# Attention of a hybrid decoder layer: probabilities transposed by TensorE into PSUM instead of by VectorE blocks and SBUF-to-SBUF transfers

## The chip, the cores and the metric

The kernel runs on one core of one Trainium2 chip. The metric is the device time of one execution in microseconds; the median of three runs before the change is 1390.19 us.

## What is computed

One decoder layer, float32, sequence 1024, width 1024, batch 1. The normalised input is projected to queries (8 heads of 64), to keys and values of 2 groups, to gates and to a convolution branch. Each head attends in three ways, and a gate weighs each of them:

```python
p_c = masked_softmax(s_c, dist_c >= 0)              # 63 compressed keys
o_c = jnp.einsum('bgrqn,bngd->bqgrd', p_c, vc)
...
p_s = masked_softmax(s_s, dist_s >= 0)              # selected blocks: all 16, so plain causal attention
o_s = jnp.einsum('bgrqnl,bgqnld->bqgrd', p_s, vs_sel)
...
p_w = masked_softmax(s_w, mask_w)                   # window of 512
o_w = jnp.einsum('bgrqs,bsgd->bqgrd', p_w, vwc)
o = gc[..., 0:1] * o_c + gc[..., 1:2] * o_s + gc[..., 2:3] * o_w
...
mix = jnp.concatenate([attn_out, conv_out], axis=-1) @ w_out
x = x + gate1 * mix
h2 = rms_norm(x, norm2) * (1 + scale2) + shift2
ff = jnp.square(jax.nn.relu(h2 @ w_ff1)) @ w_ff2
return x + gate2 * ff
```

The scores have the queries on the partitions, so the probabilities must be transposed before they can be multiplied with the values.

## The kernel before

All activations stand with channels on partitions and tokens along the columns, in two halves of 512 tokens. Every matmul operand is split into a high part rounded to fp32r and the remainder (`hi`, `lo`), and a product is three matmuls, `hi*hi + hi*lo + lo*hi` (`mm3`, L460). Weights are loaded in pieces of 256 KB into three staging buffers, cast by ScalarE or GpSimd and subtracted by VectorE (`weights`, L536).

No engine's order is written out by hand. Each helper of `Plan` (`mm` L305, `pet` L312, `copy` L330, `tt` L341, `dvt` L381, `dma` L388) records an operation with a cost in ns. `issue` (L272) runs a list scheduler over what was recorded: `_forward` (L154) places operations by priority on the engines and on one model of the DMA engines, `_backward` (L237) renews the priorities, and the best of eight passes is written out as each engine's fixed order. The plan's costs thus decide only the order; on the chip each engine takes its instructions in that order and waits where an operand is late. All plain transfers go through the SP queue, in order.

The first part (projections, compressed keys and values, conv and attention, output projection, the first 30 tiles of the MLP's first product for the first 512 tokens) is one such plan, the rest of the MLP a second one.

Attention goes in 12 steps (`supers`, L1172). A step is a pair of heads `hp` with query blocks `m` of 256 tokens: four steps with m = 0 and 1, then eight with m = 2 or 3. Within a step:

- `row` (L934), for each of 128 queries and a head: scores by TensorE into the banks `sc`, a table added and the maximum taken by VectorE (`ttr`, L373), exponentials by ScalarE, scaling by gate and denominator on GpSimd or ScalarE. Then `dvt` (L382) transposes 32x32 blocks on VectorE into the tile `Tt`.
- `shuffle` (L1011): 16 SBUF-to-SBUF transfers move the 32-row blocks from `Tt` to `Dt`, which completes the transpose. `Tt` and `Dt` exist once.
- `pv` (L1017): for pieces of `Dt` a ScalarE copy makes `hi` and a VectorE subtraction `lo` (both SBUF to SBUF); each matmul of values with probabilities covers both heads and, where causality allows, both query tiles, so most have 512 moving columns and the others 256. They sum in the bank `po` or `stb`. The result goes to `d_attn` in DRAM (`flush_pv`, L1174) and is read back by `load_mix` (L1101).

TensorE's other work while attention runs: the conv products (`conv_fills`, L1089) during the first four steps; then `first_half` (L1129), the output projection, second norm and first MLP product for the first 512 tokens. Its residual sum goes to `d_x1` in DRAM and is read back twice. After the last step the output projection of the second half follows, then its norm, then the second plan.

## Time and profile before

| | |
|---|---|
| median of 3 runs | 1390.19 us (1389.83 to 1394.37) |
| profiled execution, its own time | 1398.64 us |
| span from first to last instruction in that execution | 1396.7 us |
| mean granted TensorE clock | 0.955 |
| 0 to 225 us | projections, compressed keys, values, queries |
| 225 to 853 us | attention, with conv and the first half's products between |
| 853 us to the end | the MLP plan |

The profile is of one execution. Busy times of TensorE count a matmul from its start to the modelled end of its result, and matmuls overlap; what a matmul costs in a stream is read from the distance between starts. The granted clock is 1.0 at the higher of TensorE's two levels (2.4 GHz) and 0.5 at the lower (1.2 GHz); a value between is a mean over the stretch.

### The profile page before, as it was taken

The page shows a single profiled execution, that of the slowest core. Times are in us where ns is not written, and L with a number is a line of the kernel's source. Part 1 is how long each engine was busy: PE and PEld are TensorE (multiplying, and loading weights), DVE is VectorE, ACT ScalarE, POOL GpSimd, SP SyncE. Part 2 cuts the span into 40 slices and gives each one's busy share as a digit, 9 for nine tenths or more (in the row PEclk, how much of TensorE's full clock was granted, in tenths as well). Part 3 has the DMA queues.
Part 4 walks back from the last instruction along what each step waited for, and adds up shares of the span by engine and source line. Part 5 has one row for each costly group of instructions (what it writes and reads, how often), then busy time and mean ns, then how long its engine had stood idle before and what let it go on. Part 6 is the DMA issues. An engine that isn't in the chain of part 4 may idle for free.

```text
span 1396.7 us, 17048 instructions
## 1 busy us (share of the span) xinstructions
PE 1278.2 (92%) x5608; PEld 1031.4 (74%) x5608; DVE 835.7 (60%) x2019; ACT 619.0 (44%) x1206; POOL 131.2 (9%) x244
## 2 busy tenths in 40 slices
PE   6998999889878898987886997999999999999998
PEld 2777788668756777776765785878888888888887
DVE  6986969779778795776784647433432343143222
ACT  5775656646646475766673635411221032013200
POOL 0000003222312121212120000000000000000000
PEclk9999999889989999998988998999999999999999
DMA  9578866886686856879669714432321232122131
GB/s 327 174 195 226 262 216 208 213 197 177 192 222 172 247 165 185 231 186 222 173 165 258 225 46 157 126 124 76 106 91 61 68 114 63 58 91 91 31 121 61
DMA packets 110029, 220.66 MB, mean 158 GB/s; under 512 B 14841, under 2 KB 40994, under 8 KB 109428
## 3 DMA queue, kind: packets, MB, share of 16 engines
q1 hardware_dynamic: 106196, 204.76, 51.1%
q0 software_dynamic: 3744, 14.81, 3.7%
q8 instruction: 44, 0.72, 0.2%
q14 instruction: 45, 0.37, 0.1%
HBM read 151.77 MB, written 36.80 MB: 135 GB/s over the span
## 4 chain that ended last, share of the span: by engine, by line
PE 59%; DMA 14%; DVE 13%; SPq 7%; ACT 4%; issue 3%; POOL 0%; DVEq 0%; ACTq 0%; POOLq 0%
PE pd L310 37%; PE fa L310 10%; PE sc L310 9%; SPq L394 7%; DMA FA<-FA 5%; DVE RA L345 3%; DVE FA L382 3%; ACT FA L328 2%; PE stb L310 2%; DVE FA L356 2%; DVE FA L345 2%; DMA d_x<-FA 2%; DVE FA L375 1%; ACT RA L334 1%; PE po L310 1%
## 5 line engine op out<-in xcount | busy, mean ns | idle before, releaser
L334 ACT CAST RA<-FA 128x512 fp32r<-128x512 f32 (+4 forms) x323 | 231.5, 738 | 585.6 <-PE pd L310 286.3
L345 DVE TENSOR_TENSOR RA<-FA,RA 128x512 fp32r<-128x512 f32 (+5 forms) x407 | 319.7, 809 | 185.1 <-PE pd L310 95.0
L310 PE MATMUL fa<-RA 128*128 128x512 f32 (+1 forms) x1384 | 398.9, 407 | 18.2 <-DVE RA L345 8.0
L310 PE MATMUL sc<-RA 128*128 128x512 f32 (+6 forms) x1328 | 319.0, 368 | 22.5 <-DVE mx L375 8.9
L310 PE MATMUL pd<-hid,RA 128*128 128x512 f32 x1344 | 336.2, 389 | 0.0
L310 PEld LDWEIGHTS fa<-RA 128*128 128x128 f32 (+1 forms) x1384 | 267.1, 197 | 81.9 <-DVE RA L345 13.8
L310 PEld LDWEIGHTS pd<-hid,RA 128*128 128x128 f32 x1344 | 252.2, 188 | 52.2
L310 PEld LDWEIGHTS sc<-RA 128*128 128x128 f32 x1328 | 236.3, 194 | 70.9 <-DVE mx L375 12.1
L310 PE MATMUL pd<-RA 128*128 128x512 f32 x1008 | 263.9, 393 | 8.6 <-ACT RA L334 6.0
L310 PEld LDWEIGHTS pd<-RA 128*128 128x128 f32 x1008 | 189.8, 190 | 51.7 <-ACT RA L334 6.3
L356 DVE SCALAR_TENSOR_TENSOR FA<-pd,mod,FA 128x512 f32<-128x512 f32 x64 | 46.1, 745 | 201.1 <-PE pd L310 201.1
L382 DVE STREAM_TRANSPOSE FA<-FA 128x128 f32<-128x128 f32 (+8 forms) x224 | 97.4, 481 | 60.3 <-DMA FA<-FA 53.6
L328 ACT ACTIVATE FA<-FA,nm 128x64 f32<-128x64 f32 (+6 forms) x192 | 114.1, 596 | 23.2 <-DVE nm L364 21.2
L328 ACT ACTIVATE FA<-FA 128x512 f32<-128x512 f32 (+2 forms) x147 | 88.5, 618 | 26.2 <-DVE FA L356 14.7
L310 PE MATMUL stb<-RA 128*128 128x512 f32 (+1 forms) x192 | 64.8, 398 | 26.1 <-ACT RA L334 20.1
L375 DVE CUSTOM_DVE_ANT_0 FA<-sc,FA 128x64 f32<-128x64 f32 (+5 forms) x192 | 80.3, 450 | 6.1 <-PE sc L310 5.4
L368 POOL TENSOR_SCALAR FA<-FA,cf 128x64 f32<-128x64 f32 (+8 forms) x107 | 68.5, 654 | 109.2 <-DVE cf L345 89.6
L310 PE MATMUL po<-RA 128*128 128x512 f32 (+4 forms) x164 | 50.6, 394 | 27.8 <-ACT RA L334 26.8
L310 PEld LDWEIGHTS stb<-RA 128*128 128x128 f32 x192 | 36.6, 201 | 36.7 <-ACT RA L334 21.7
L338 POOL TENSOR_SCALAR RA<-FA 128x512 fp32r<-128x512 f32 x54 | 35.2, 654 | 276.2 <-DMA FA<-in_w_ff 78.6
L310 PEld LDWEIGHTS po<-RA 128*128 128x128 f32 (+1 forms) x164 | 30.7, 206 | 38.5 <-ACT RA L334 30.1
L370 ACT ACTIVATE FA<-FA,cf 128x64 f32<-128x64 f32 (+8 forms) x85 | 50.1, 633 | 11.3 <-DVE cf L345 8.5
(121 smaller groups left out, 690.8 us busy)
## 6 DMA issues: line engine op xcount, KB each, us to landing
FA<-in_w_ff SPq DMA_DIRECT2D x64, 512.0 KB, 4.2
FA<-FA SPq DMA_DIRECT2D x128, 176.0 KB, 4.9
FA<-in_w_ada SPq DMA_DIRECT2D x64, 256.0 KB, 3.9
FA<-in_w_ff SPq DMA_DIRECT2D x60, 256.0 KB, 4.0
FA<-FA SPq DMA_DIRECT2D x64, 208.0 KB, 4.7
FA<-in_w_cols SPq DMA_DIRECT2D x34, 256.0 KB, 3.6
FA<-in_xT SPq DMA_DIRECT2D x32, 256.0 KB, 5.5
FA<-in_w_ada SPq DMA_DIRECT2D x16, 512.0 KB, 6.0
```

The costliest lines, as they stand in the source:

```text
L310: self.op([("PE", c, lambda: self.nc.tensor.matmul(out, a, b, start=start, stop=stop))], [out], [a, b])
L328: self.op([("ACT", c, lambda: self.nc.scalar.activation(out, a, func, **kw))], outs, ins)
L334: alts.append((e, 0.833 * n + (53 if ps else 93), lambda: self.nc.scalar.copy(out, a)))
L338: alts.append((e, 0.833 * n + 174, lambda: self.nc.gpsimd.tensor_scalar(out, a, 1.0, 0.0, ALU.mult, ALU.add)))
L345: alts.append((e, 1.04 * n + 68, lambda: self.nc.vector.tensor_tensor(out, a, b, op)))
L356: self.op([("DVE", 1.04 * self._n(out) + 68 + 61 * ptr, lambda: self.nc.vector.scalar_tensor_tensor(out, a, s, b, op0, op1, **kw))], [out] ...
L368: alts.append((e, 0.833 * n + 174 + 83 * ptr, lambda: self.nc.gpsimd.tensor_scalar(out, a, s1, s2, op0, op1)))
L370: alts.append((e, 0.833 * n + 93 + 93 * ptr, lambda: self.nc.scalar.activation(out, a, AF.Copy, scale=s1)))
L375: self.op([("DVE", 1.04 * self._n(out) + 75, lambda: self.nc.vector.tensor_tensor_reduce(out, a, b, 1.0, init, ALU.add, ALU.max, accum))], ...
L382: self.op([("DVE", 1.04 * self._n(out) + 68, lambda: self.nc.vector.transpose(out, a))], [out], [a])
L394: self.op([(q, c, lambda: e.dma_start(out=out, in_=a))], [out], [a], nbytes=n)
```

## The change

Each block of 128 queries by 128 keys of a row's probabilities (and the 128 by 64 of the compressed keys) is transposed by one TensorE transpose (`pet`) into a PSUM bank, up to four blocks to a bank. ScalarE copies the bank to `hi`, VectorE subtracts to `lo`, and for every block two matmuls of 128 moving columns follow, one with `hi` and one with `lo`. `Tt`, `Dt`, `dvt` and `shuffle` go. The four rows of a step's block sum in the four quarters of one bank `po`; `stb` and `sc2` become the transposes' banks, so scores have two banks (three for m of 2 or 3) in place of three (four). The attention output of the first half stays in SBUF (`at0`), that of the second half is split straight into `h[1]`; the first half's residual stays in SBUF (`x1h`). In the planner a transpose costs 110 in place of 218, an SBUF-to-SBUF transfer counts double, and every transfer ends 1000 ns later. Regions of SBUF are laid out anew, and the conv's and first half's weights share three split buffers.

```diff
                     start = t + cost + 660
-                end = dma = max(dma, start) + o.nbytes / 360.0
+                end = dma = max(dma, start) + o.nbytes * o.weight / 360.0
+                end += 1000.0
                 if e == "SP":
                     free[e] = max(t + 50, hw - cost, dma - 2500)
...
     def pet(self, out, a, ident):
-        self.op([("PE", 218.0, lambda: self.nc.tensor.transpose(out, a, ident))], [out], [a, ident])
+        self.op([("PE", 110.0, lambda: self.nc.tensor.transpose(out, a, ident))], [out], [a, ident])
 
     def act(self, out, a, func, bias=None, scale=1.0, accum=None):
         c = 0.833 * self._n(a) + (53 if self._ps(a) else 93)
...
+        self.op([(q, c, lambda: e.dma_start(out=out, in_=a))], [out], [a], nbytes=n, weight=2 if within else 1)
 
 
...
 
 
-H0, H1, WR, RAN = 0, 8192, 16384, 16384 + 7744
-AHEAD = {"pv5": 100}
-FA1N, FA2N = 13316, 14336
+H0, H1, WR, RAN = 0, 8192, 16384, 16384 + 11328
+AHEAD = {}
+FA1N, FA2N = 13316, 10752
...
 
-    d_attn = [[dtile(f"d_attn{p}{m}", 128, 256) for m in range(4)] for p in range(4)]
     d_conv = [[dtile(f"d_conv{j}{i}", 128, 512) for i in range(2)] for j in range(4)]
     d_q = [[dtile(f"d_q{p}{i}", 2, 128, 2, 2, 256) for i in range(2)] for p in range(4)]
     d_k = [dtile(f"d_k{g}", 128, KW0 + T) for g in range(2)]
     d_v = [dtile(f"d_v{g}", 128, 8, 2, 128) for g in range(2)]
-    d_x1 = dtile("d_x1", 8, 128, 512)
     d_hid = [dtile(f"d_hid{j}", 128, 512) for j in range(NFF)]
     d_row = dtile("d_row", NH, TROW)
     d_tab = [dtile(f"d_tab{i}", 128, TROW) for i in range(NH)]
...
     gates = ctile("gates", 8, 24)
-    vc = [[ctile(f"vc{g}{s}", 128, dtype=R) for s in range(2)] for g in range(2)]
+    vc = [ctile(f"vc{g}", 128, dtype=R) for g in range(2)]
...
-                for s in range(2):
-                    r = slice(64 * s, 64 * s + 63)
-                    P.copy(vc[g][s][r, 0:64], cv)
-                    P.sub(vc[g][s][r, 64:128], cv, f32(cvh))
+                P.copy(vc[g][0:63, 0:64], cv)
+                P.sub(vc[g][0:63, 64:128], cv, f32(cvh))
 
     def values():
 
...
     tabt = [(pbr(T), pbr(128), pbr(128)) for _ in range(2)]
-    Tt0, Dt0 = (Region(FA2, c, c + 5632)(4, 22, 64) for c in (0, 6656))
-    Tt1, Dt1 = Br(4, 26, 64), Cr(4, 26, 64)
-    ot = Region(FA2, 13312, FA2N - 512)(4, 4, 32)
-    ot_r = Rot([(ot[0:64], 64), (ot[64:128], 0)])
+    Gr = Region(FA2, 0, FA2N - 640)
+    x1h, at0 = [Gr(512) for _ in range(8)], [Gr(512) for _ in range(4)]
+    ot_r, ada_acc, ada_r = Gr.rot(2, 256), Gr(512), Gr.rot(3, 512)
     cg_t, z_t, t1_t = ([Dr(n) for _ in range(2)] for n in (512, 514, 512))
 
     Wr = Region(RA, WR, RAN)
-    fw0_r, hl0_r = Wr.rot(2, 2, 512), Wr.rot(3, 4, 2, 64)
+    fw0_r, hl_r, kall0, q0_r, vt0 = Wr.rot(3, 2, 512), Wr.rot(8, 512), Wr(KC0 + T), Wr.rot(2, 2, 2, 256), Wr(4, 2, 128)
     Wr = Region(RA, RAN - 4160, RAN)
-    kall0, q0_r, vt0 = Wr(KC0 + T), Wr.rot(2, 2, 2, 256), Wr(4, 2, 128)
-    Wr, Hr = Region(RA, RAN - 4160, RAN), Region(RA, H1, H1 + 8192)
-    kall1, q1_r, vt1 = Wr(KW0 + T), Wr.rot(2, 2, 2, 256), Hr(8, 2, 128)
-    fwx_r, hl1_r = Region(RA, WR, WR + 3328).rot(3, 2, 512), Hr.rot(6, 4, 4, 64)
-    half0 = kall0, KC0 + 512, q0_r, vt0, hl0_r, 2, Rot(sc_t[0:3]), Tt0, Dt0
-    half1 = kall1, KW0, q1_r, vt1, hl1_r, 4, Rot(sc_t), Tt1, Dt1
-    po_r, fa_r = Rot([t.rearrange("p (a q n) -> p a q n", a=4, q=2) for t in (po_t, stb)]), Rot(fa_t)
+    fwx_r, kall1, q1_r, vt1 = Rot(fw0_r.t), Wr(KW0 + T), Wr.rot(2, 2, 2, 256), Region(RA, H1, H1 + 2048)(8, 2, 128)
+    half0 = kall0, KC0 + 512, q0_r, vt0, Rot(sc_t[0:2])
+    half1 = kall1, KW0, q1_r, vt1, Rot([sc_t[0], sc_t[1], sc_t[3]])
+    tp_r, po_r, fa_r = Rot([sc_t[2], stb]), Rot([po_t]), Rot(fa_t)
     pb = [0]
 
     def prow(w):
...
@@ -985,68 +975,26 @@
...
             P.ts(s[:, rs[br]], s[:, rs[br]], cf[:, br:br + 1], 0.0, mult, add, engs=("POOL", "ACT"))
-
-        ic = slice(hl * 32, hl * 32 + 32)
-
-        def tr(off, kt0, n, hs, step=2):
-            src = s[:, off + kt0 * 128:off + (kt0 + n) * 128].rearrange("p (k b j) -> p k b j", b=4, j=32)
-            dst = Tt[:, :, T0 + hs:T0 + hs + step * (n - 1) + 1:step, ic].rearrange("p b k i -> p k b i")
-            P.dvt(dst, src)
-
-        nF, _ = geom(m)
-        off = 64 + nf
-        P.dvt(Tt[:, 2 * qp:2 * qp + 2, T0 + 4 * m + 2, ic], s[:, 0:64].rearrange("p (b j) -> p b j", j=32))
-        tr(64, 0, qt + 1, qp)
-        if m >= 2:
-            if qp == 0:
-                tr(off, 0, 5, nF)
-            else:
-                tr(off, 0, 4, nF + 3)
-                tr(off, 4, 1, nF + 1)
-        else:
-            tr(off, 0, 2 * m + 1, nF + qp)
-            if qp == 1:
-                tr(off, 2 * m + 1, 1, nF + 2 * (2 * m + 1))
-
-    def shuffle(n, full):
-        *_, Tt, Dt = half1 if full else half0
-        for a in range(4):
-            for b in range(4):
-                P.dma(Dt[32 * b:32 * b + 32, a, 0:n], Tt[32 * a:32 * a + 32, b, 0:n])
-
-    def pv(hp, m, T0, o):
-        g = hp // 2
-        nF, nW = geom(m)
-        _, _, _, vt, hl_r, ns, _, _, Dt = half1 if m >= 2 else half0
-        vF, vW = ([vt[:, k, b] for k in range(2 * m + 2)] for b in range(2))
-        jobs = [(2 * kt, 4, [(vF[kt], 0, 2, 0), (vF[kt + 1], 2, 2, 0)]) for kt in range(0, 2 * m, 2)]
-        jobs.append((4 * m, 4, [(vF[2 * m], 0, 2, 0), (vc[g][0], 2, 1, 0), (vc[g][1], 2, 1, 1), (vF[2 * m + 1], 3, 1, 1)]))
-        if m >= 2:
-            w = 2 * m - 4
-            jobs.append((nF, 4, [(vW[w], 0, 1, 0), (vW[2 * m + 1], 1, 1, 1), (vW[w + 1], 2, 2, 0)]))
-            jobs.append((nF + 4, 4, [(vW[w + 2], 0, 2, 0), (vW[w + 3], 2, 2, 0)]))
-            jobs.append((nF + 8, 2, [(vW[w + 4], 0, 2, 0)]))
-        else:
-            jobs += [(nF + 2 * kt, 4, [(vW[kt], 0, 2, 0), (vW[kt + 1], 2, 2, 0)]) for kt in range(0, 2 * m, 2)]
-            jobs.append((nF + 4 * m, 3, [(vW[2 * m], 0, 2, 0), (vW[2 * m + 1], 2, 1, 1)]))
-        if ns == 2:
-            jobs = [(hs + c0, min(2, nh - c0), [(v, c - c0, n, qp) for v, c, n, qp in uses if c // 2 * 2 == c0])
-                    for hs, nh, uses in jobs for c0 in range(0, nh, 2)]
-        acc = po_r()
-        for ji, (hs, nh, uses) in enumerate(jobs):
-            hi, lo = hl_r(), hl_r()
-            src = Dt[:, :, T0 + hs:T0 + hs + nh]
-            P.copy(hi[:, :, 0:nh], src, ("ACT",))
-            P.sub(lo[:, :, 0:nh], src, f32(hi[:, :, 0:nh]), EW)
-            for ui, (v, c, n, qp) in enumerate(uses):
-                last = ji == len(jobs) - 1 and ui == len(uses) - 1
-                oo = acc[:, :, qp:qp + n]
-                P.mm(oo, v, hi[:, :, c:c + n], ji == 0 and ui == 0, False)
-                P.mm(oo, v, lo[:, :, c:c + n], False, last)
-        o, p0 = o
-        ac, oo = acc.rearrange("p a q (h i) -> p a (q h) i", h=2), o.rearrange("d c a i -> d a c i")
-        P.copy(oo, ac[p0:p0 + 64])
-        P.tt(oo, ac[64 - p0:128 - p0], oo, add)
+        vF, vW = ([vt[:, k, b] for k in range(qt + 1)] for b in range(2))
+        return [(s[:, rs[1]][:, 128 * k:128 * k + 128], vF[k]) for k in range(qt + 1)] + \
+            [(s[:, rs[0]], vc[hp // 2][0:64])] + \
+            [(s[:, rs[2]][:, 128 * (k - w0):128 * (k - w0) + 128], vW[k]) for k in range(w0, qt + 1)]
+
+    def pv(oo, blocks):
+
+        parts = [b for b in blocks if b[0].shape[-1] == 128]
+        parts = [[b for b in blocks if b[0].shape[-1] < 128]] + [parts[i:i + 4] for i in range(0, len(parts), 4)]
+        for gi, part in enumerate(parts):
+            n, w = 128 * len(part), part[0][0].shape[-1]
+            tp, hi, lo = tp_r()[0:w, 0:n], hl_r()[0:w, 0:n], hl_r()[0:w, 0:n]
+            for i, (p, _) in enumerate(part):
+                P.pet(tp[:, 128 * i:128 * i + 128], p, ident)
+            P.copy(hi, tp)
+            P.sub(lo, tp, f32(hi))
+            for i, (_, v) in enumerate(part):
+                c = slice(128 * i, 128 * i + 128)
+                P.mm(oo, v, hi[:, c], gi + i == 0, False)
+                P.mm(oo, v, lo[:, c], False, gi == len(parts) - 1 and i == len(part) - 1)
 
     def products(groups, rot, h):
 
...
-        t_r = Rot(z_r.t + [t2])
         for k in range(8):
-            x = t_r()
-            P.dma(x, d_x1[k])
-            norm2_apply(k, x, x, y, h0)
+            norm2_apply(k, t_r(), x1h[k], y, h0)
             yield
-        t_r = Rot(t_r.t + [ca, tb])
+        t_r = Rot(t_r.t + [ca])
         rot = fwx_r
...
 
-    def flush_pv(hp, jobs):
-        outs = {m: ot_r() for m, _ in jobs}
-        for m, T0 in jobs:
-            pv(hp, m, T0, outs[m])
-        for m, _ in jobs:
-            for qp in range(2):
-                dst = d_attn[hp][m][:, qp * 128:qp * 128 + 128].rearrange("(h d) t -> d h t", h=2)
-                P.dma(dst, outs[m][0][:, 2 * qp:2 * qp + 2].rearrange("d h a i -> d h (a i)"))
+    def attention(hp, m, q):
+
+        acc = po_r()
+        o = at0[hp][:, 256 * m:256 * m + 256] if m < 2 else ot_r()
+        for i in range(4):
+            pv(acc[:, 128 * i:128 * i + 128], row(hp, m, i % 2, i // 2, q))
+        for hl in range(2):
+            r, c = slice(64 * hl, 64 * hl + 64), slice(256 * hl, 256 * hl + 256)
+            P.copy(o[r], acc[r, c])
+            P.tt(o[r], acc[64 - 64 * hl:128 - 64 * hl, c], o[r], add)
+        if m >= 2:
...
         for m in ms:
             q = q_r()
             P.dma(q.rearrange("p h i t -> p (h i t)"), d_q[hp][m // 2][m % 2].rearrange("p h i t -> p (h i t)"), "POOL")
-            for i in range(4):
-                row(hp, m, i // 2, i % 2, q, T0)
-            jobs.append((m, T0))
-            T0 += sum(geom(m))
-        P.group = f"shuffle{u}"
-        shuffle(T0, full)
-        P.group = f"pv{u}"
-        flush_pv(hp, jobs)
+            attention(hp, m, q)
...
-    tmp = Rot([FA2[:, 512 * i:512 * i + 512] for i in range(6)])
-    sacc, y1 = FA2[:, 3072:3584], FA2[:, 3584:4096]
+    tmp, sacc, y1 = Rot(at0), Gr(512), Gr(512)
     wt_r = Region(RA, RAN - 4160, RAN).rot(4, 2, 512)
...
     rsqrt_neg2(y1, tmp(), stb)
     for k in range(8):
         norm2_apply(k, tmp(), x1[k][1], y1, h[1])
     for c in range(8):
-        P.dma(x1[c][0], d_x1[c])
+        P.dma(x1[c][0], x1h[c])
     P.issue()
     if dbg:
         for i in range(2):
-            for s in range(2):
-                nc.sync.dma_start(out=dbg["vc"][i, s], in_=f32(vc[i][s]))
```

## Rows read from the trace of the kernel before

**Rows 1.** The page: engines' busy us, share, instructions; granted clock in 40 slices.

```profile
PE 1278.2 (92%) x5608; PEld 1031.4 (74%) x5608; DVE 835.7 (60%) x2019; ACT 619.0 (44%) x1206; POOL 131.2 (9%) x244
...
PEclk9999999889989999998988998999999999999999
```

**Rows 2.** Stretches: length, busy PE, PEld, DVE, ACT, POOL, clock, DMA share, GB/s.

```profile
0.00:225.00 225.00, 200.79 (x909) 155.95 (x910) 177.58 (x428) 140.84 (x277) 12.88 (x40) 0.96 0.77 236
225.00:853.00 628.00, 539.67 (x2338) 433.11 (x2337) 467.57 (x1322) 371.83 (x791) 118.28 (x204) 0.92 0.71 190
...
870.00:1397.00 527.00, 520.77 (x2300) 428.54 (x2298) 179.13 (x251) 102.15 (x134) 0.00 (x0) 1.00 0.27 86
```

**Rows 3.** Timeline of SP, first shuffle: start, length, what, count.

```profile
240.69 13.54 SPq L394 DMA_DIRECT2D FA<-FA  x16
```

**Rows 4.** Timeline of TensorE behind it; in brackets, idle before.

```profile
259.24 0.64 PE L310 MATMUL sc<-RA 128*128 128x64 f32 x2 [5.05 <-DVE mx L375]
```

**Rows 5.** Stretches around that shuffle.

```profile
250.00:262.00 12.00, 5.83 (x24) 4.07 (x22) 4.46 (x23) 2.95 (x8) 4.06 (x10) 0.78 1.08 252
262.00:268.00 6.00, 5.78 (x17) 4.60 (x18) 4.79 (x13) 2.55 (x5) 2.06 (x6) 0.58 0.98 334
```

**Rows 6.** Waits, 225 to 853 us: total us, times, longest.

```profile
DVE FA L382 <- DMA FA<-FA: 53.6, 16, 7.2
```

**Rows 7.** TensorE by shape, 225 to 853 us: count, busy, mean ns, idle before.

```profile
L310 PE MATMUL fa<-RA 128*128 128x512 f32 x1205 | 343.8, 412 | 16.5 <-DVE RA L345 6.3 <-DVE FA L356 3.7 <-ACT FA L328 3.1
L310 PE MATMUL sc<-RA 128*128 128x512 f32 x504 | 143.6, 401 | 7.8 <-DVE mx L375 3.9 <-DMA RA<-d_q 1.8 <-ACT RA L334 1.4
L310 PE MATMUL stb<-RA 128*128 128x512 f32 x136 | 51.3, 430 | 22.6 <-ACT RA L334 20.1 <-DVE RA L345 2.4
L310 PE MATMUL po<-RA 128*128 128x512 f32 x88 | 34.7, 460 | 27.6 <-ACT RA L334 26.8 <-DVE RA L345 0.8
L310 PE MATMUL sc<-RA 128*128 128x128 f32 x76 | 14.7, 266 | 0.0
...
L310 PE MATMUL po<-RA 128*128 128x256 f32 x40 | 9.2, 304 | 0.1
...
L310 PE MATMUL fa<-FA,bones 128*128 128x512 f32 x2 | 1.0, 592 | 0.0
```

**Rows 8.** Timeline of TensorE, six matmuls and a seventh (shapes merge).

```profile
232.23 0.39 PE L310 MATMUL fa<-RA 128*128 128x512 f32 x1
232.46 0.39 PE L310 MATMUL sc<-RA 128*128 128x512 f32 x1
232.69 0.39 PE L310 MATMUL fa<-RA 128*128 128x512 f32 x1
232.91 0.62 PE L310 MATMUL sc<-RA 128*128 128x128 f32 x3
233.37 0.39 PE L310 MATMUL fa<-RA 128*128 128x512 f32 x1
```

**Rows 9.** TensorE by shape, 232.66 to 233.35 us.

```profile
L310 PE MATMUL sc<-RA 128*128 128x128 f32 x2 | 0.3, 248 | 0.0
```

**Rows 10.** Timeline of TensorE at two of four transposes (L313).

```profile
110.67 0.94 PE L310 MATMUL sc<-RA 128*128 128x280 f32 x6
111.44 0.38 PE L313 MATMUL fa<-FA 126*128 126x126 f32 x2
111.58 1.03 PE L310 MATMUL sc<-RA 128*128 128x280 f32 x6
```

**Rows 11.** VectorE groups: the 32x32 transposes, an addition out of PSUM.

```profile
L382 DVE STREAM_TRANSPOSE FA<-FA 128x128 f32<-128x128 f32 (+8 forms) x224 | 97.4, 481 | 60.3 <-DMA FA<-FA 53.6 <-DMA FA<-in_w_ada 1.6 <-ACT FA L370 1.4
...
L345 DVE TENSOR_TENSOR FA<-fa,FA 128x512 f32<-128x512 f32 x10 | 6.8, 678 | 0.1
```

**Rows 12.** Stretches before attention and at the MLP's start.

```profile
150.00:225.00 75.00, 73.75 (x348) 60.82 (x347) 63.46 (x159) 42.04 (x84) 6.89 (x14) 1.00 0.78 244
...
836.00:868.00 32.00, 23.41 (x86) 17.70 (x86) 23.16 (x40) 17.39 (x26) 0.00 (x0) 0.84 0.44 137
```

More of the change, by code (lines that the diff above doesn't have):

```diff
@@ L39 @@
 class Op:
-    __slots__ = ("alts", "idx", "preds", "succs", "nbytes", "past", "end", "group", "port")
+    __slots__ = ("alts", "idx", "preds", "succs", "nbytes", "past", "end", "group", "port", "weight")
     def __init__(self, alts, idx, nbytes):
@@ L114, in _covers, with op @@
         return True
-    def op(self, alts, outs, ins, nbytes=0, port=()):
+    def op(self, alts, outs, ins, nbytes=0, port=(), weight=1):
         o = Op(alts, len(self.ops), nbytes)
+        o.weight = weight
         o.port = port
@@ L393, in dma @@
         c = 1040.0 if q == "POOL" else 475.0 if a.space == DRAM else 650.0
-        self.op([(q, c, lambda: e.dma_start(out=out, in_=a))], [out], [a], nbytes=n)
+        within = a.space != DRAM and out.space != DRAM
+        self.op([(q, c, lambda: e.dma_start(out=out, in_=a))], [out], [a], nbytes=n, weight=2 if within else 1)
 class Rot:
@@ L552, in hymba_layer @@
     wfs_r, sq_r = Br.rot(3, 384), Region(FA1, 8192, FA1N - 1024).rot(6, 512)
-    y_t, sa_t = ([Br(512) for _ in range(2)] for _ in range(2))
-    wa_r = Cr.rot(5, D)
+    y_t = [Br(512) for _ in range(2)]
+    wa_r = Br.rot(5, D)
+    sc = Br(2, 512)
+    scv = sc.rearrange("p a n -> p (a n)")
     wf = [Region(RA, WR + 3072 * i, WR + 3072 * i + 3072)(8, 384) for i in range(2)]
@@ L593, in hymba_layer @@
     for g in range(2):
-        for s in range(2):
-            P.zero(f32(vc[g][s]))
+        P.zero(f32(vc[g]))
     P.ts(sl, ct, -1.0, 80.0, mult, amin)
@@ L1097, in conv_fills, with out_proj @@
             yield
-    order = (4, 5, 6, 7, 0, 1, 2, 3)
     def load_mix(hf, k, t, hi, lo):
-        k = order[k]
-        if k >= 4:
-            P.dma(t, d_conv[k - 4][hf])
-        else:
-            for i in range(2):
-                P.dma(t[:, i * 256:i * 256 + 256], d_attn[k][2 * hf + i])
+        if k < 4:
+            P.dma(t, d_conv[k][hf])
+        else:
+            t = at0[k - 4]
         P.copy(hi, t, ("ACT", "DVE"))
         P.sub(lo, t, f32(hi), EW)
-    def out_proj(hf, tmp, rot, mix, banks, done):
-        for k in range(8):
-            load_mix(hf, k, tmp(), mix[0][:, k], mix[1][:, k])
+    def out_proj(rot, mix, banks, done):
         for c in range(8):
@@ L1131, in first_half @@
         (ca, t2), (ta, tb) = cg_t, t1_t
-        z_r = Rot([z[:, 0:512] for z in z_t])
+        t_r = Rot([z[:, 0:512] for z in z_t] + [t2, tb])
         def done(c, a):
-            x = z_r()
+            x = x1h[c]
             P.dma(x, xT[c, :, 0:512])
-            P.stt(t2, a, mod[:, 16 + c:17 + c], x, mult, add)
-            P.dma(d_x1[c], t2)
-            add_square(c, ta, ca, t2)
+            P.stt(x, a, mod[:, 16 + c:17 + c], x, mult, add)
+            add_square(c, ta, ca, x)
         tmp = Rot([ca, ta, tb])
@@ L1229, in hymba_layer @@
     P.group = "half1"
-    out_proj(1, tmp, wt_r, h[1], Rot(sc_t), done_second)
+    for k in range(4):
+        load_mix(1, k, [ada_acc, *ada_r.t][k], h[1][0][:, k], h[1][1][:, k])
+    out_proj(wt_r, h[1], Rot(sc_t), done_second)
     P.mm(stb, f32(bones), sacc, True, True)
@@ L1239, in hymba_layer @@
         for i in range(2):
-            for s in range(2):
-                nc.sync.dma_start(out=dbg["vc"][i, s], in_=f32(vc[i][s]))
+            nc.sync.dma_start(out=dbg["vc"][i], in_=f32(vc[i]))
         nc.sync.dma_start(out=dbg["gates"], in_=gates)
         for p in range(4):
-            for m in range(4):
-                nc.sync.dma_start(out=dbg["attn"][p * 128:p * 128 + 128, m * 256:m * 256 + 256], in_=d_attn[p][m])
             for m in range(2):
@@ L1262, in hymba_layer @@
         wh_r, wl_r = Rot([w5[0], w5[2], w5[4]]), Rot([w5[1], w5[3]])
-        Wr = Region(RA, WR + 1024, WR + 3072)
-        hids = [Wr(512) for _ in range(4)] + [ff.tile([128, 512], R, name=f"hid{i}") for i in range(28)]
+        Wr = Region(RA, WR + 1024, RAN - 4160)
+        hids = [Wr(512) for _ in range(12)] + [ff.tile([128, 512], R, name=f"hid{i}") for i in range(20)]
         hid = [[[hids[16 * hf + 2 * j + i] for hf in range(2)] for j in range(8)] for i in range(2)]
```

24 lines of the change are left out of this document (11 added, 13 removed).

## The prediction

> **What bounds the kernel now.** I read the page first, then busy time by stretch, then the timelines around one step of attention, then the waits, and last the matmuls by shape. The page shows TensorE busy 92% of the span, with a granted clock that dips only in the middle [rows 1]. By stretch there are three parts [rows 2]. Before 225 us matmuls cover 200.79 of 225 us. From 870 us they cover 520.77 of 527 us at clock 1.00: that part is TensorE's alone, and the change adds nothing to it. Between, in 225 to 853 us, they cover 539.67 of 628 us at a mean clock of 0.92. All that the change touches lies there.
>
> That stretch loses its time at the shuffles. The first one holds the SP queue for 13.54 us with its 16 issues [rows 3]. While it runs VectorE, ScalarE and TensorE are busy 4.46, 2.95 and 5.83 of 12 us, the DMA share is 1.08, and the clock falls: 0.78 in that stretch and 0.58 in the next 6 us [rows 5]. TensorE idles 5.05 us before its next score [rows 4]. The pattern repeats for the 12 steps. Over the stretch the 32x32 transposes wait 53.6 us for shuffles to free their tile [rows 6], and TensorE waits 26.8 us in `po` and 20.1 us in `stb` for the `hi` copies, which wait for the shuffled data [rows 7].
>
> Busy time counts overlapping and half-speed matmuls alike, so I need the work itself: count times start-to-start cost at the full clock. Three steps of a stream of 512-column matmuls take 232.23 to 232.91, or 0.227 us each. From 232.23 to 233.37 there are four of them and two of 128 columns [rows 8, 9]: 1.14 - 4 x 0.227 = 0.232, or **0.116 us for a 128-column matmul**. It is half of a 512-column one, not a quarter. Every matmul carries its own load of 128 weight columns (5608 loads for 5608 matmuls [rows 1]), and a short matmul doesn't hide the next load.
>
> Work of the stretch [rows 7]: 1205 + 504 + 136 + 88 = 1933 of 512 columns at 0.227 make 438.8 us. The 256-column ones of `pv` are four groups, two of 40 (`po` and `stb`) and two of 32 with the compressed values, 144 in all; at 0.116, half of the long ones, that is 16.7. The twelve other shapes, from the 76 of 128 columns to the last with two, come to 36 at these prices by columns, none under 0.116. The code issues 224 long ones in `pv` where 216 are recorded: 2 more. Sum **493 us in 628**: 135 us are idle time, slow clock and small gaps.
>
> **The change part by part.**
>
> *Removed on TensorE:* the old `pv`, 224 x 0.227 + 144 x 0.116 = 67.5 us.
>
> *Added on TensorE, transposes:* a row of query tile qt has qt + 1 full blocks, one compressed and min(qt, 4) + 1 of the window; over eight tiles 36 + 8 + 30 = 74, times 8 heads 592. The kernel has four transposes of nearly this shape. Two of them start at 111.44 and the next matmul at 111.58, but that next run of six lasts 1.03 where the run before lasted 0.94 [rows 10], so the pair costs 0.14 + 0.09 = 0.23, or 0.115 each. The ends are 0.07 (the starts alone) and 0.14 (twice that); I take 0.115, which counts the delay behind. 592 x 0.115 = 68 us.
>
> *Added on TensorE, products:* each block gives two matmuls (hi, lo) of 128 columns, 1184 x 0.116 = 137.3 us. The columns streamed are the same as before; what was one matmul for two heads and two tiles is now four, each with its own weight load.
>
> The Trainium skill states another price in "TensorE: Matmul & The Clock Gate", Back-to-back issue gap: in a stream of load and matmul pairs about 81 ns for 128 columns. By that the products would cost 96 us as an estimate, the work would be 590 us, and the rest of my sum unchanged would end at 1375. The row says 116 ns here, and the measurement decides.
>
> *New sum:* 493 - 67.5 + 68 + 137.3 = **631 us of work in a stretch that now lasts 628**. This is the core of the forecast: the loss that goes (135 us at the most) is what the new work adds (138 us). What decides is how much TensorE still idles.
>
> *Idle that stays.* Just before attention, with projections and many VectorE subtractions, matmuls cover 73.75 of 75 us [rows 11]: 1.7% idle. With short chains of softmax between, I take 3%, with 1.7 and 5 as ends: 631 / 0.97 = 651. The handover to the MLP (the norm's chain) leaves 8.6 us of 32 idle and a clock of 0.84 [rows 11]; nothing there changes, and 5 us of it falls into the stretch. Together 656, or 28 us more than 628.
>
> *New waits.* A group of up to four blocks must pass a ScalarE copy and a VectorE subtraction out of PSUM (0.678 us for 512 columns [rows 12]) before its matmuls. There are 152 such groups and 64 of one compressed block, 216. Had TensorE nothing else queued, the subtractions alone would hold it 216 x 0.678 = 146 us at the most; behind them stand conv or MLP products, of which these 628 us hold 1205 [rows 7], so I price them at nothing beyond the 3%. If the products run out early, that cover is gone. With one bank `po` each block's sum must be emptied before the next block's first product; two transposing banks bound how far TensorE runs ahead; scores lose one bank. All are 1 to 2 us of other work to be found, 16 times or per group, and go into the 5% end.
>
> *Off the path.* VectorE loses 97.4 us of transposes [rows 12] and stays at the same number of columns in the subtractions: 467.57 [rows 2] falls to about 385 of 650, since reading PSUM and the smaller pieces cost a little more. ScalarE keeps its casts' columns; 371.83 of 628 [rows 2] is no bound either. The DMA loses the shuffles, `d_attn` and a part of `d_x1`; weights land earlier, but nothing in the sum waits for them. The SP queue loses the 13.5 us blocks. These gains are real and worth nothing once TensorE is full.
>
> *Planner.* Every transfer counted 1 us later and the new layout reorder the whole first plan. The nearest row is the first stretch, 24 us not covered in 225 [rows 2]: I bound this at 10 us either way and take 0. The plan prices a 128-column matmul at 0.4375 x 128 + 3 = 59 ns, half the row's price, so TensorE falls behind the plan by up to 1184 x 0.057 = 67 us; then the others wait for it rather than it for them, which speaks for the small idle share.
>
> *Time.* The profiled execution took 1398.64 us, 1396.7 of it the span and 1.9 around it; plus 28 is 1426.6. It was 0.6% above the median, so times 1390.19 / 1398.64: **1418 us**.
>
> **Rivals.**
>
> *TensorE never waits* (0.18). The stretch is 631 + 5, and the first 225 us give back up to 10 since weights meet no shuffle: about 1388. For it speaks the optimistic plan; against it that no stretch with softmax rows in it runs without gaps. About half of this case lies over 0.3% faster and half within 0.3%, which is about what a measurement of this kernel can tell from no change.
>
> *The loads hide, and it is faster* (0.09). Place: the pair of products with the same values and the interleaving with long matmuls. If a 128-column matmul cost a quarter of 0.227, or 0.057, the work would be 493 - 67.5 + 68 + 67.5 = 561, the stretch 561 / 0.97 + 5 = 583, the time 1398.64 - 45, in median terms 1345. It decides from 0.094 us per product, where the stretch comes out at 628. For it: in the old `pv`, too, hi and lo follow each other with the same values. Against it: there every matmul has its load as well [rows 1], and the row's two stand between long matmuls and still cost 0.116 each.
>
> *The clock falls* (0.11). Today it sits at the lower level for about (1 - 0.92) / 0.5 x 628 = 100 us of the stretch [rows 2], always behind stalls like that of rows 5. If TensorE's clock fell in the stretches of transposes and short products, 205 us in all, half of them at half speed would cost up to 100 us more; I take 50 on top of the forecast: 1468. In the rows, the two transposes of rows 10 leave no mark, but they are two. The Trainium skill bears on this in "TensorE: Matmul & The Clock Gate", Part 4: PE-mode transpose: it says that the full clock does not engage for TensorE's transposes. No run here shows a stretch of transposes.
>
> **How the numbers follow.** The forecast has 0.62, the rivals 0.18, 0.09 and 0.11. Low end: transposes at 0.07 (604 us of work), 1.7% idle, plus 5: 620, 8 less than today, and 3 of the possible 10 in the first stretch: 1388 in the profile's terms, 1379. High end: transposes at 0.14 (646), 5% idle, plus 5: 685, 57 more: 1456, so 1447. The hidden loads and the clock lie outside, 0.20 together. Faster: 0.09 + 0.08 = 0.17. Same: 0.10 + 0.02 of the forecast's low edge = 0.12. Slower: 0.71.
>
> **What would show it.** In the profile after: no transfer from FA to FA of the shuffle's kind; no 5 us idle of TensorE followed by a low clock at each step; clock near 1.0 through attention; VectorE down by about 80 us; 592 transposes, and streams of short products at 0.11 to 0.12 us from start to start; TensorE covered to 95% or more from 225 us on, with attention's stretch 15 to 55 us longer and the MLP's 527 us unchanged. I am wrong if short products run at 0.06 to 0.09, if the work ahead of 225 us moves by more than 10 us, or if the clock is low in long runs of transposes.

## The result and the profile after

The changed kernel takes 1434.66 us (median of 4 runs, 1433.45 to 1437.25) where the kernel before takes 1391.85 beside it. The ratio is 1.0306, with a 95% interval of 1.0283 to 1.033: slower by 3.1%, or 42.8 us. The forecast was 1418, slower, with a range from 1379 to 1447.

The profiled execution took 1435.77 us, with a span of 1434.0 where it was 1396.7: 37.3 us more. The page of the changed kernel (busy us, share of the span and instructions; then the granted clock in 40 slices) answers to [rows 1]:

```profile
PE 1397.4 (97%) x7016; PEld 1141.2 (80%) x7016; DVE 781.6 (55%) x1928; ACT 644.8 (45%) x1362; POOL 114.3 (8%) x221
...
PEclk8999999999999999999999998999999999999999
```

TensorE is now busy 97% of the span, and the clock's dips in the middle are gone but for one at the handover to the MLP. By stretch (length; busy PE, PEld, DVE, ACT and POOL with counts; clock, DMA share, GB/s), with columns as in [rows 2], the changed kernel reads:

```profile
0.00:225.00 225.00, 201.23 (x918) 155.75 (x918) 176.96 (x425) 146.56 (x310) 15.63 (x43) 0.95 0.77 244
225.00:853.00 628.00, 626.49 (x3610) 518.31 (x3609) 388.88 (x1193) 371.04 (x883) 98.67 (x179) 1.00 0.34 112
907.00:1434.00 527.00, 523.00 (x2309) 430.54 (x2308) 181.82 (x255) 103.10 (x134) 0.00 (x0) 1.00 0.27 87
...
225.00:884.50 659.50, 655.19 (x3733) 541.13 (x3731) 406.64 (x1221) 383.85 (x902) 98.67 (x179) 1.00 0.33 108
884.50:1434.00 549.50, 541.00 (x2368) 444.30 (x2368) 198.02 (x283) 114.42 (x151) 0.00 (x0) 0.99 0.28 90
```

The first 225 us carry the same work at the same cover, and the last 527 us are as before. The first matmul of the MLP starts at 844.2 us in the kernel before and at 884.6 in the changed one. So from 225 us to that point it is 619.2 against 659.5 us: all of the loss, 40.3 us, lies in the stretch that the change touches (the end gives 3 back). The same stretch of the kernel before, to its own end:

```profile
225.00:844.00 619.00, 537.57 (x2333) 431.82 (x2331) 458.57 (x1306) 363.04 (x779) 118.28 (x204) 0.92 0.71 190
```

What the change set out to remove is gone: the clock goes from 0.92 to 1.00, the DMA share from 0.71 to 0.34, and TensorE stays uncovered for 4.3 us in 659.5 instead of 81 in 619. VectorE is busy 389 of the 628 us where it was 468 [rows 2]; up to the MLP's first matmul, which is the same work in both kernels, it falls from 459 to 407 us, by 52. The stretch is longer all the same. The waits of 225 to 853 us in the changed kernel (who waits <- for whom: us in total, times, longest), to be laid beside [rows 6]:

```profile
POOL FA L370 <- DVE cf L347: 147.9, 48, 11.7
POOL RA L340 <- PE fa L312: 110.2, 19, 13.9
...
DVE FA L377 <- PE sc L312: 59.4, 61, 3.5
DVE RA L347 <- ACT RA L336: 57.1, 68, 3.4
ACT RA L336 <- PE sc L315: 54.8, 43, 3.7
```

The wait of VectorE for the shuffles [rows 6] has left. The other engines now wait for TensorE's scores (`sc`, L312) and its transposes (`sc`, L315), and TensorE hardly for them: from 225 us on the kernel is bound by TensorE's work.

By shape, TensorE from 225 to 890 us in the changed kernel (count, busy us, mean ns, idle before; L315 is the transposes):

```profile
L312 PE MATMUL fa<-RA 128*128 128x512 f32 x1207 | 408.4, 424 | 1.1 <-DVE RA L347 1.1
L312 PE MATMUL po<-RA 128*128 128x128 f32 x1048 | 196.8, 264 | 0.1
L312 PE MATMUL sc<-RA 128*128 128x512 f32 x511 | 166.7, 409 | 0.0
L315 PE MATMUL stb<-FA,FA 128*128 128x128 f32 x305 | 77.3, 283 | 0.0
L315 PE MATMUL sc<-FA,FA 128*128 128x128 f32 x212 | 51.3, 281 | 0.0
...
L312 PE MATMUL po<-RA,vc 64*128 64x128 f32 x124 | 36.1, 316 | 0.2 <-DVE FA L347 0.2
```

Against [rows 7], the idle time before `po` and `stb` (27.6 and 22.6 us) has become 0.1 and none. The last line is the one that the forecast had not priced apart: products of the compressed block, whose weights have 64 rows. Here is the timeline of TensorE around two of them (start, busy, operation, count), and then that of its weight loads (in brackets, idle before):

```profile
702.43 0.39 PE L312 MATMUL fa<-RA 128*128 128x512 f32 x1
702.66 0.62 PE L312 MATMUL sc<-RA 128*128 128x512 f32 x2
703.12 0.39 PE L312 MATMUL fa<-RA 128*128 128x512 f32 x1
703.35 0.27 PE L315 MATMUL sc<-FA,FA 128*128 128x128 f32 x1
703.55 0.33 PE L312 MATMUL po<-RA,vc 64*128 64x128 f32 x1
703.81 0.50 PE L312 MATMUL sc<-RA 128*128 128x512 f32 x1
704.15 0.64 PE L312 MATMUL fa<-RA 128*128 128x512 f32 x2
704.72 0.33 PE L312 MATMUL po<-RA,vc 64*128 64x128 f32 x1
704.97 0.50 PE L312 MATMUL fa<-RA 128*128 128x512 f32 x1
```

```profile
703.55 0.18 PEld L312 LDWEIGHTS po<-RA,vc 64*128 64x128 f32 x1 [0.29 <-issue]
703.81 0.19 PEld L312 LDWEIGHTS sc<-RA 128*128 128x128 f32 x1
703.92 0.43 PEld L312 LDWEIGHTS fa<-RA 128*128 128x128 f32 x2
704.72 0.18 PEld L312 LDWEIGHTS po<-RA,vc 64*128 64x128 f32 x1 [0.37 <-issue]
704.97 0.19 PEld L312 LDWEIGHTS fa<-RA 128*128 128x128 f32 x1
```

Two 512-column matmuls start at 704.15 and take 2 x 0.227, so the product could start at 704.60; it starts at 704.72, and the next matmul 0.25 us behind it. Its weight load starts with it at 704.72, after the loading port has idled for 0.37 us, while elsewhere loads run under earlier matmuls. Of the 128, 63 stand behind a 512-column matmul, which then takes 0.327 us from start to start in the median instead of 0.227; the product itself takes 0.254 in the median (0.164 in the 19 cases where another product of 64 rows follows). Together that is 0.100 + 0.254 = **0.354 us where the forecast took 0.116**, and as an estimate for all of them 128 x 0.238 = 30 us.

### The profile page after: what moved, and what is told of

Its sections match the earlier page's. It is cut to its first block, busy times and chain, and to the rows that moved or that the text cites. A ratio compares the mean times of both kernels' runs of the same rounds, so it can differ in the third digit from the quotient of the medians.

```text
span 1434.0 us, 19643 instructions
## 1 busy us (share of the span) xinstructions
PE 1397.4 (97%) x7016; PEld 1141.2 (80%) x7016; DVE 781.6 (55%) x1928; ACT 644.8 (45%) x1362; POOL 114.3 (8%) x221
## 4 chain that ended last, share of the span: by engine, by line
PE 90%; DMA 4%; DVE 2%; ACT 1%; issue 1%; SPq 1%; DVEq 0%; ACTq 0%
PE pd L312 37%; PE fa L312 23%; PE sc L312 16%; PE po L312 9%; PE stb L315 3%; PE sc L315 2%; DMA d_tab<-d_row 1%; ACT FA L330 1%; DVE FA L358 1%; DVE RA L347 1%; DMA FA<-in_w_cols 1%; SPq L397 1%; DMA FA<-in_w_ada 1%; DVE FA L347 0%; DMA FA<-in_xT 0%
## 5 line engine op out<-in xcount | busy, mean ns | idle before, releaser
L312 PE MATMUL fa<-RA 128*128 128x512 f32 (+1 forms) x1384 | 463.3, 419 | 1.1 <-DVE RA L347 1.1
L312 PE MATMUL pd<-RA 128*128 128x512 f32 x1392 | 413.8, 393 | 7.4 <-ACT RA L336 4.3
L336 ACT CAST RA<-FA 128x512 fp32r<-128x512 f32 (+5 forms) x235 | 163.0, 708 | 491.8 <-PE pd L312 286.3
L312 PE MATMUL sc<-RA 128*128 128x512 f32 (+6 forms) x1328 | 357.3, 371 | 12.0 <-DVE RA L338 9.8
L347 DVE TENSOR_TENSOR RA<-FA,RA 128x512 fp32r<-128x512 f32 (+5 forms) x327 | 246.7, 773 | 166.6 <-PE pd L312 95.5
L312 PEld LDWEIGHTS pd<-RA 128*128 128x128 f32 x1392 | 262.4, 190 | 66.3 <-ACT RA L336 5.0
L312 PE MATMUL pd<-hid,RA 128*128 128x512 f32 x960 | 310.4, 389 | 0.0
L312 PEld LDWEIGHTS fa<-RA 128*128 128x128 f32 (+1 forms) x1384 | 250.6, 190 | 42.6 <-DVE RA L347 1.6
L312 PEld LDWEIGHTS sc<-RA 128*128 128x128 f32 x1328 | 236.1, 191 | 54.2 <-DVE RA L338 10.6
L312 PEld LDWEIGHTS pd<-hid,RA 128*128 128x128 f32 x960 | 180.2, 188 | 37.4
L312 PE MATMUL po<-RA 128*128 128x128 f32 (+1 forms) x1092 | 206.4, 266 | 0.1
L312 PEld LDWEIGHTS po<-RA 128*128 128x128 f32 (+1 forms) x1092 | 185.4, 193 | 18.0 <-DVE RA L347 0.5
L377 DVE CUSTOM_DVE_ANT_0 FA<-sc,FA 128x512 f32<-128x512 f32 (+5 forms) x192 | 82.8, 455 | 43.3 <-PE sc L312 41.9
L315 PE MATMUL stb<-FA,FA 128*128 128x128 f32 (+1 forms) x332 | 84.3, 283 | 0.0
```

What stands on the lines that cost most here:

```text
L312: self.op([("PE", c, lambda: self.nc.tensor.matmul(out, a, b, start=start, stop=stop))], [out], [a, b])
L315: self.op([("PE", 110.0, lambda: self.nc.tensor.transpose(out, a, ident))], [out], [a, ident])
L336: alts.append((e, 0.833 * n + (53 if ps else 93), lambda: self.nc.scalar.copy(out, a)))
L347: alts.append((e, 1.04 * n + 68, lambda: self.nc.vector.tensor_tensor(out, a, b, op)))
L377: self.op([("DVE", 1.04 * self._n(out) + 75, lambda: self.nc.vector.tensor_tensor_reduce(out, a, b, 1.0, init, ALU.add, ALU.max, accum))], ...
```

## The experiments

The theory to be tested: TensorE's work sets the time; short products and transposes cost 0.116 us each whatever they do, and nothing off TensorE matters. Rivals: VectorE's way through PSUM holds the products back; the planner's order does; the clock. The first four kernels have one time each, from a chip where the kernel before took 1385.82 us; by the ratio 1.0306 the changed kernel would take 1428.2 there. The three of them that are made from the changed kernel are compared with that.

**One product per block in place of two** (`hi_only`).

```diff
-                P.mm(oo, v, hi[:, c], gi + i == 0, False)
-                P.mm(oo, v, lo[:, c], False, gi == len(parts) - 1 and i == len(part) - 1)
+                P.mm(oo, v, hi[:, c], gi + i == 0, gi == len(parts) - 1 and i == len(part) - 1)
```

> The changed kernel without the 592 products of the low part (the output lacks that part); transposes, copies and subtractions stay. Theory (TensorE is full from 225 us on, and a short product costs its price): 592 x 0.116 to 0.130 us less, so 1358 to 1366 us against 1434.66. Rival (the way through PSUM, that is copy, subtraction and one summing bank, sets the pace): within 10 us of 1435, since that way is as long as before. Rival (loads of weights hide behind the products): 592 x 0.057 = 34 us less, 1401.

Measured: 1362.36 us, 66 less than 1428.2, for 592 products fewer: 0.111 each. The time follows TensorE's work. With the 64 among them that cost 0.354 priced as such, 84 us of work went, so 18 us of it did not come back as time.

**Each transpose twice** (`pet_twice`).

```diff
-                P.pet(tp[:, 128 * i:128 * i + 128], p, ident)
+                for _ in range(2):
+                    P.pet(tp[:, 128 * i:128 * i + 128], p, ident)
```

> The changed kernel with every transpose done twice into the same place. Theory: 592 x 0.113 to 0.115 us more, 1501 to 1503, clock as before (0.987). Rival (transposes bring TensorE's clock down): over 1530, and a mean clock under 0.97 with long stretches at the lower level.

Measured: 1497.69 us, 69.5 more than 1428.2, or 0.117 us per added transpose (63 more than 1434.66 taken as it is, 0.106). The page and the stretch of this kernel show what the clock does with 1184 transposes:

```profile
PEclk8999999999999999999999999999999999999999
...
225.00:948.00 723.00, 719.84 (x4330) 600.41 (x4328) 413.65 (x1218) 388.70 (x897) 96.94 (x174) 1.00 0.32 102
```

The clock is 1.00. That the clock falls under transposes is refuted, and their price stands.

**Each subtraction out of PSUM twice** (`sub_twice`).

```diff
-            P.sub(lo, tp, f32(hi))
+            for _ in range(2):
+                P.sub(lo, tp, f32(hi))
```

> The changed kernel with each of the 216 subtractions out of PSUM done twice: 111 us more of VectorE, which now has 389 of 628 us in attention. Theory: within 10 us of 1434.66, since VectorE is off the path. Rival (the way through PSUM sets the pace): 50 to 111 us more, 1485 to 1546.

Measured: 1449.77 us, 15 more than 1434.66 or 21.5 more than 1428.2. Its first 225 us and its stretch:

```profile
0.00:225.00 225.00, 194.98 (x899) 151.46 (x900) 178.34 (x460) 150.43 (x330) 18.46 (x52) 0.94 0.73 229
225.00:898.00 673.00, 666.45 (x3751) 548.44 (x3749) 485.16 (x1397) 383.35 (x887) 95.06 (x169) 1.00 0.35 111
```

VectorE is busy 485.16 us where it was 406.64 in that stretch of the changed kernel: 79 us more, and 15 to 21 us, about a quarter of it, show up in the time. "Within 10" was missed: VectorE is not wholly off the path. That it is the bound is refuted; it would have cost about all of the 79. A part of the loss lies before 225 us, where attention has begun and VectorE is busy 79% of the time: TensorE covers 6 us less there than the 201.23 of the changed kernel, with 19 matmuls fewer, and these come later. In the stretch itself TensorE is uncovered for 6.6 us instead of 4.3. Where the rest lies the trace doesn't say.

**The kernel before without the shuffle's transfers** (`no_shuffle`; `pv` then reads the unshuffled tile).

```diff
-        for a in range(4):
-            for b in range(4):
-                P.dma(Dt[32 * b:32 * b + 32, a, 0:n], Tt[32 * a:32 * a + 32, b, 0:n])
+        return
...
-        _, _, _, vt, hl_r, ns, _, _, Dt = half1 if m >= 2 else half0
+        _, _, _, vt, hl_r, ns, _, Dt, _ = half1 if m >= 2 else half0
```

> The kernel before without its 192 SBUF-to-SBUF transfers: the products read the tile of the 32x32 transposes itself, so the probabilities stand in the wrong order and the output is not the reference's. Theory (the shuffles' stalls are nearly all of what attention lost): 493 us of TensorE's work at 4.5% idle, plus 5, against 628, so 107 us less: about 1285, at most 1305 as VectorE fills up. Rival (weights that land late, or VectorE's transposes, hold TensorE as well): under 60 us less, 1330 or more.

Measured: 1298.43 us, 87.4 less than 1385.82, where 107 less was expected. Its stretch:

```profile
225.00:743.00 518.00, 505.14 (x2340) 412.03 (x2339) 462.09 (x1360) 367.59 (x801) 115.83 (x190) 0.99 0.51 163
```

The forecast's 493 us of priced work come out in 518 us, with VectorE busy as long as before (462 against 459 us). The stretch is 101 us shorter than the 619 of the kernel before. So of the 126 us that it lost there about 100 were the shuffles' transfers; the run doesn't tell whether by the SP queue, the single tile or the time of the transfers. The sum of TensorE's work from [rows 7 to 9] can be too low by 5% at the most. The 32x32 transposes on VectorE, which are still in this run, cost at most the 25 us that are left.

**Two heads in one product** (`pairs`). From here on times are medians, with the ratio to the kernel before and its interval. One product now streams 256 columns, a block of each of two heads with the same values, so that half as many weight loads carry the same columns.

```diff
+        blocks = list(zip(*pair))
...
-            for i, (_, v) in enumerate(part):
-                c = slice(128 * i, 128 * i + 128)
+            for i, two in enumerate(part):
+                c, v = slice(256 * i, 256 * i + 256), two[0][1]
...
-        for i in range(4):
-            pv(acc[:, 128 * i:128 * i + 128], row(hp, m, i % 2, i // 2, q))
+        for qp in range(2):
+            pv(acc[:, 256 * qp:256 * qp + 256], [row(hp, m, qp, hl, q) for hl in range(2)])
```

> The changed kernel, but the two heads of a query tile go together: two blocks of each head to a PSUM bank, and each product covers both heads, 256 columns in place of 128. 592 products in place of 1184, transposes the same. Theory: 1184 x 0.116 to 0.130 becomes 592 x 0.118, so 67 to 84 us less than 1434.66: 1351 to 1368, faster than the kernel before (1391.85) by 1.7 to 3%. Rival (the way through PSUM sets the pace, or two rows that must wait for each other cost as much as they give): 1420 or more.

Measured: 1368.62 us, ratio 0.9817 (0.9791 to 0.9843): 4.9% of 1390, or 68 us, below the changed kernel. 592 products fewer (64 of them with 64 rows) give what `hi_only` gave, though every column is still streamed. So a 256-column product costs nearly what a 128-column one costs. The traces say the same: where two stand behind each other, 256-column products start 0.118 us apart here in the median (107 pairs, mean 0.130), and 128-column ones 0.111 us in the changed kernel (390 pairs, mean 0.106). It is not the columns that are paid for. That it is the weight load fits the loads shown above, two of which start 0.11 us apart (703.81 and 703.92), but no run changed the load alone. The stretch of `pairs`, 66 us shorter than the 659.5 of the changed kernel at nearly the same cover:

```profile
225.00:818.00 593.00, 587.65 (x3151) 482.34 (x3149) 402.93 (x1215) 381.71 (x877) 110.14 (x197) 0.99 0.38 119
```

**The planner's price of a short matmul** (`true_cost`), and **the planner's old prices** (`old_plan`: transposes, transfers and the 1 us behind each transfer as before), both in the changed kernel.

```diff
-        c = max(0.4375 * n + 3, 58.0)
+        c = max(0.4375 * n + 3, 116.0)
```

> The changed kernel with 116 ns as the planner's least price of a matmul in place of 58, which is what the trace shows; only the order of the instructions changes. Theory (TensorE is full, its order matters little): within 10 us of 1434.66. Rival (the plan's wrong price put instructions into a bad order): 15 to 35 us less, 1400 to 1420.

```diff
-                end += 1000.0
...
-        self.op([("PE", 110.0, lambda: self.nc.tensor.transpose(out, a, ident))], [out], [a, ident])
+        self.op([("PE", 218.0, lambda: self.nc.tensor.transpose(out, a, ident))], [out], [a, ident])
...
-        self.op([(q, c, lambda: e.dma_start(out=out, in_=a))], [out], [a], nbytes=n, weight=2 if within else 1)
+        self.op([(q, c, lambda: e.dma_start(out=out, in_=a))], [out], [a], nbytes=n, weight=1)
```

> The changed kernel with the planner's prices of before: a transpose 218 in place of 110, no 1000 ns on a transfer's end, SBUF-to-SBUF transfers counted once. Theory: within 10 us of 1434.66. Rival (the planner's new prices carry a part of the result): 15 us or more away, either way.

Measured: `true_cost` 1431.59 us, ratio 1.027 (1.0242 to 1.0298), whose interval overlaps that of the change; `old_plan` 1449.85, ratio 1.0402 (1.0358 to 1.0445), about 13 to 15 us slower than the change, where "within 10" was expected. So the planner's price of the products makes no difference that shows, and its new prices of transposes and transfers, which are part of the change, are worth about 1%. The stretch of `old_plan` is 670 us at clock 0.99, ten more than after:

```profile
225.00:895.00 670.00, 664.32 (x3752) 546.53 (x3750) 408.81 (x1212) 381.91 (x890) 101.36 (x178) 0.99 0.34 110
```

Which of the three prices it is wasn't tried.

**The kernel before with the new prices of transfers** (`before_plan`).

```diff
-                end = dma = max(dma, start) + o.nbytes / 360.0
+                end = dma = max(dma, start) + o.nbytes * (2 if o.within else 1) / 360.0
+                end += 1000.0
...
```

> The kernel before with the change's prices of transfers (SBUF-to-SBUF counted twice, every end 1000 ns later), and nothing else of the change. Theory (the shuffles hold the SP queue and the single tile whatever the order): within 15 us of 1391.85. Rival (the stalls came from an order that expected the transfers too early): 25 us or more faster.

Measured: 1390.56 us, ratio 0.9989 (0.9965 to 1.0014). So the new prices of transfers take nothing off the stalls at the shuffles.

**The compressed block over 128 rows** (`full_rows`). The rows 64 to 127 of `vc` hold zeros, so multiplying them with whatever stands beside the compressed probabilities adds nothing. The block keeps its own group.

```diff
-            [(s[:, rs[0]], vc[hp // 2][0:64])] + \
+            [(s[:, 0:128], vc[hp // 2], 1)] + \
...
```

> The changed kernel, but the block of the compressed keys is transposed as 128 columns (its own 64 and the 64 that stand behind it in the row) and multiplied by the compressed values over 128 rows, of which those past 62 are zero; it keeps its own group, so only the shape of 64 transposes and 128 products differs. In the changed kernel's trace the next matmul starts 252 to 257 ns after such a product of 64 rows, and the product itself starts 326 ns after a 512-column one in place of 227: 0.35 us each where the forecast had 0.116. Theory (the 64 rows cost that, as their weights are not loaded ahead): 128 x 0.237 = 30 us less than 1434.66, about 1404. Rival (these products wait for their split operands): within 8 us of 1434.66.

Measured: 1404.25 us, ratio 1.0111 (1.0088 to 1.0133): 27 us (by the ratios) to 30 us less than the changed kernel, for the same number of matmuls and columns. Its stretch and its products by shape:

```profile
225.00:854.50 629.50, 623.78 (x3728) 537.98 (x3727) 407.42 (x1223) 388.19 (x908) 97.45 (x176) 0.99 0.35 114
```

```profile
L312 PE MATMUL po<-RA 128*128 128x128 f32 x1056 | 198.4, 265 | 0.5 <-ACT RA L336 0.5
...
L312 PE MATMUL po<-RA,vc 128*128 128x128 f32 x128 | 28.9, 255 | 0.4 <-DVE FA L347 0.4
```

The products with `vc` now take 255 ns of busy time, less than the others (they were at 316), and the stretch is 30 us shorter. The weight loads of these products, first in the changed kernel and then here (count, busy us, mean ns, idle time of the loading port before them):

```profile
L312 PEld LDWEIGHTS po<-RA,vc 64*128 64x128 f32 x128 | 22.0, 183 | 27.6 <-issue 19.7 <-ACT FA L330 2.1 <-ACT RA L336 0.9
```

```profile
L312 PEld LDWEIGHTS po<-RA,vc 128*128 128x128 f32 x128 | 23.5, 191 | 3.7 <-ACT RA L336 1.0
```

The port's idle time before the loads of 64 rows, 27.6 us in all, is gone with 128 rows. That settles the 30 us: they are the price of weights with 64 rows.

**Both together** (`pairs_rows`), and with the planner's price of 116 ns (`pairs_rows_cost`).

> Two heads together as in the run pairs, and the compressed block over 128 rows as in full_rows, now in the same groups of four as the others. Theory: 64 products of 64 rows lose 0.237 us each, 15 us less than the 1368.62 of pairs: about 1353, 2.8% under the kernel before (1391.85). Rival: no change from 1368.62.

> The run pairs_rows with 116 ns as the planner's least price of a matmul. Theory: as the run true_cost gave 3 us, 0 to 6 us less than pairs_rows. Rival (the order matters more once TensorE is less full): 10 us or more away.

Measured: 1348.18 us, ratio 0.9707 (0.9676 to 0.9738), and 1346.95, ratio 0.9694 (0.9668 to 0.9719). Both are 3% faster than the kernel before; the price makes no difference that shows. Against `pairs` the 128 rows give 20 us by the times and 15 by the ratios, where 15 was expected. The stretch of `pairs_rows`, and its products with `vc`:

```profile
225.00:797.00 572.00, 567.37 (x3158) 482.01 (x3157) 403.10 (x1212) 374.95 (x860) 118.98 (x211) 1.00 0.39 123
```

```profile
L312 PE MATMUL po<-RA,vc 128*128 128x256 f32 x64 | 17.8, 306 | 0.0
```

## Why the prediction was right, and where its sum was off

**What bounds the kernel, and the core of the sum: right.** It said that 135 us were lost in the stretch, that the change would win most of them back, and that the new work would eat them up. In numbers: up to the MLP's first matmul 619.2 us held 493 of work, so 126 us were lost there (the 135 count to 853 us). That stretch grew by 40; the new work is 138 us as forecast and 30 that were missed, 168; so 128 us came back, which is all of the loss within the error of the prices. `no_shuffle` shows where about 100 of them came from, and `hi_only` and `pet_twice` show that the time follows the count of short matmuls.

**Price of a short product: right for 1056 of the 1184, wrong for 128.** The forecast took 0.116 us for every product. That row [rows 8, 9] has weights of 128 rows, as every shape in [rows 7] has; the products of the compressed block have 64 rows in the new layout, and cost 0.354. This is the mis-sized term, 30 us, shown by `full_rows`. The trace of before has no such product, so the forecast could have given it a bound of its own; it didn't list it.

**Price of a transpose: right.** 0.115 was taken, 0.106 to 0.117 measured, for a second one right behind the first.

**Idle that stays: too large.** The forecast had 3% of idle time, 20 us, and 5 us for the handover, against 631 us of work. Work of 631 + 30 = 661 us came out in 659.5. The same holds in `full_rows`: 631 us of work in 629.5. Prices that are read to about 0.01 us leave 12 us either way in 1184 products, but at the lowest prices measured, 0.111 for a product and 0.106 for a transpose, the work is 651 us and 1.3% is left. The cover says the same: 0.7% uncovered after, and 0.9% in `full_rows`, where 3% was taken. It is a lower bound, since a 512-column matmul is busy for 0.39 us and the next starts 0.227 us behind it [rows 8], so a short wait leaves no gap. The nearest stretch of before, at 1.7% [rows 12; the prediction's text names that group and the VectorE groups of rows 11 the other way round], was the better end. The idle share comes back when TensorE has less to do: `no_shuffle` is 518 us for 493 of work, and `pairs_rows` 572 for 562 (631 less 592 x 0.116). So a forecast of idle time has to ask how full the engine will be, and the price of an edit falls short by that: `pairs_rows` took away 99 us of priced work and won 83 (0.0599 of 1390).

The two errors, 30 too little and about 20 too much, leave the forecast 10 us short of the profile's difference (28 against 37.3). That they cancel in part is luck. The rest up to the 17 us between 1418 and 1434.66 is that the profiled execution of before lay 0.6% above the median of its runs, and that of after 0.1%.

**Off the path: right for the bound, too low for VectorE's time.** VectorE was to fall by about 80 us, to about 385 us of the stretch; it is busy 406.64 of 659.5, 52 less than before. The 97.4 us of transposes went [rows 11]. But the 216 subtractions out of PSUM take 111 us, while those between SBUF tiles fell by 80 and 73 us. Reading PSUM isn't the reason, as 512 columns take 0.686 us from there and took 0.691 from SBUF; there are more and smaller pieces. Nor is VectorE without effect: `sub_twice` shows that about a quarter of added VectorE time counts.

**Planner: not nothing.** The forecast took 0, bounded by 10 us. `old_plan` shows that the new prices give 13 to 15 us back; they are in the result. That TensorE falls behind its plan was argued as a reason for little idle time; `true_cost` takes that lag out of the plan and the time stays, so that reason was not needed. What is saved by keeping the attention output and the residual in SBUF, and what the bank that the scores lost costs, no run shows by itself.

**The rivals.** TensorE never waits: nearly right in its condition, as TensorE is covered to 99.3%, but its 1388 lacks the 30 us of the 64-row products, and counts on up to 10 us from the first 225 us, which hold the same work at the same cover as before [rows 2]. The loads hide: refuted by 0.111 us per product in `hi_only`, above the 0.094 from which it decides. The clock falls: refuted, 1.00 in the stretch and in `pet_twice`.

## What to carry to other kernels

Where an engine is stalled, its lost time is a budget: before moving work onto it, price that work start to start, and see whether it fits. A matmul of 128 columns cost nearly as much here as one of 256, so batch what shares the same weights (here two heads) until the moving side is 256 columns or more. Where weights have 64 rows, try 128 with zeros. These two edits turned a change that cost 3.1% into one that gains 3%.
